# Scores of two tiles in one bank per head, weight blocks that wait for step 8 of the down product, and pooling steps that leave out one product's slot

## The chip, the cores and the metric

The kernel runs on one core of a Trainium2 chip. The metric is the device time of one execution in microseconds (us), as the median of several runs. The core's engines are TensorE (PE in the profile; PEld is its weight load), VectorE (DVE), ScalarE (ACT), GpSimd (POOL) and SyncE (SP), which here only issues DMAs. TensorE's results go to eight banks of PSUM, 512 fp32 numbers per partition each.

## What is computed

One decoder layer on 1024 tokens of width 1024, all in fp32 (cut to its structure):

```python
h = x + 0.5 * swiglu(rms_norm(x, ffn1_norm), w1, w3, w2)          # inner width 2816
u = rms_norm(h, mix_norm)
proj = u @ w_in                       # q, k, v: 768 each; pool: 512; two gates: 1024 each
y_attn = dilated_mixture_attention(q, k, v) @ w_branch_attn       # 3 groups x 4 heads of 64
y_pool = multiscale_pool(pz, pool_w, pool_scale) @ w_branch_pool  # trailing means over 2, 4, 8, 16
merged = sigmoid(gate_a) * y_attn + sigmoid(gate_b) * y_pool
h = h + merged @ w_out
h = h + 0.5 * swiglu(rms_norm(h, ffn2_norm), w1, w3, w2)
return rms_norm(h, final_norm)
```

The attention works on blocks of 128 queries against their own block of keys and the block before it, in three groups of dilation 1, 4 and 16. The three groups' outputs are combined by their softmax denominators.

## The kernel before

Every number is split into a rounded high part (`hi`) and the rest (`lo`), and each product of two numbers is three matmuls, hi by hi, hi by lo and lo by hi (`three`). ScalarE makes the high parts, VectorE and POOL the low parts. The large matrix products are done with seven products of half-size matrices in place of eight, on sums and differences of the quarters. `ORDER` gives the order of the seven products: 1, 6, 2, 7, 5, 4, 3. The order in which instructions are issued is written out by hand: each engine runs its own instructions in the order of the program, and waits for the others by semaphores.

The stages follow each other: entry and first FFN's up product, its down product, the projection `w_in` (the mix stage), attention with the pooling branch's product in between, merge and `w_out`, and the second FFN.

**Down product** (`Down`, lines 727 to 860). The seven products are cut into six steps each, 42 in all; a step multiplies one or two blocks of 128 rows for four tiles of tokens, as `d_f` (line 814). The left side of a step, `g_f`, are sums that the up product has put into DRAM (`gs_f`); `load` (line 753) brings a step's sums back three steps ahead. `begin`, two steps ahead, splits the sums into `ahi_f` and `alo_f` and the weights into `bhi_f` and `blo_f` (`split`, lines 767 and 771). Every fourth low part is POOL's. The right side are blocks of the weights `w2`, or sums and differences of two blocks (`s_f1w`, `s_f2w`, line 789).

The blocks come through a `Stream` (lines 42 to 92): a list of pieces that are loaded in order as soon as `room` says so. Most pieces share a ring of seven tiles `raw`. The pieces numbered in `APART` (13, 14, 22, 23, 37 and 38) have places apart, in the two spare tiles `g`, and `room` allows two of them at a time. A piece that finds no room holds up all pieces behind it.

**Mix stage** (lines 1058 to 1460). It makes 19 outputs in turn, `MIX`: for each of the three groups two halves of q and k and one of v, then gates with two pooling items between them. Each output is seven products `u_mixm` (line 331). In slot `k` of the main loop the operands of product `k + 2` are made, product `k` is issued, and the result of product `k - 1` is taken from its bank by `Mix.out` (lines 1082 to 1101; `y_m`). Results 1 and 5 are taken ahead of the operands. Finished outputs and the split of late weights go on as jobs in the list `later`: at the end of a slot each job that is due does one step, up to its next `yield`, and says how many slots to wait. The job of a pooling item is `window` (lines 1167 to 1210): running sums (`pw`), subtraction of the token, split into `pd_hi` and `pd_lo` (lines 1192 and 1193), then the group's product `pm` (line 1200) and the store.

**Attention** (lines 1605 to 1900). 48 tiles, each of two heads by 128 queries, go in 24 iterations `q` of two tiles. An iteration issues, on PE: the scores `s` of both tiles (line 1624), the transposes `tp` of the exponents of iteration `q - 1` (line 1671), a piece of the pooling branch's product `yp` (line 1763), the values' product `o` of iteration `q - 2` (line 1704). VectorE gathers `o` of `q - 3` (line 1727), masks and reduces the scores (line 1642, `e<-s,mask`) and makes the low part of the transposed exponents (`elo`, line 1686); ScalarE does the exponents (line 1651) and the high part (`ehi`, line 1683). In four of the later iterations `house` also advances the combination of the first two heads (`combine`, lines 1736 to 1744): PE transposes the factors into a bank `fa` (line 1605), VectorE multiplies the gathered outputs by it (`o<-o,fa`, line 1736).

Four banks have the tag `mm` and four the tag `acc`, and each tag's banks are given out in rotation. `s` and `fa` take banks of `mm`; `tp`, `yp`, `o` of the values' product and `pm` take banks of `acc`. A tile of scores takes two banks, one for each head, and uses 128 or 256 of the 512 columns of each.

Of the kernel before, what the change touches and what calls it, by code (L numbers as in the profile page):

```python
# [16 lines left out]
P = 128  # L17
# [8 lines left out]
HD = 64  # L26
SC = HD ** -0.5
GROUPS = 3
# [18 lines left out]
class Stream:  # L47


    def __init__(self, nc, pool):  # L50
        self.nc, self.pool = nc, pool
        self.pieces, self.tiles = [], {}
        self.depth = self.n_loaded = self.n_used = self.n_back = self.end = 0
        self.apart, self.n_apart = set(), 0

    def room(self):
        if self.n_loaded in self.apart:
            return self.n_apart < 2
        return self.n_loaded - self.n_apart < self.n_back + self.depth
# [78 lines left out]
def tile_block(  # L138
# [69 lines left out]
    raws = Stream(nc, keep)  # L208
# [515 lines left out]
    class Down:  # L724
# [3 lines left out]
        def __init__(self, name, sums, half_tile, pair):  # L728
# [7 lines left out]
            self.right, self.apart = {}, set()  # L736
            downs.append(self)

        def size(self, i):
# [81 lines left out]
        def run(self, pool, after, tick=None):  # L821
# [6 lines left out]
            for i, (m, s) in enumerate(self.steps):  # L828
# [23 lines left out]
                if i + 3 < n:  # L852
                    self.load(i + 3)
                if i + 2 < n and not ahead:
                    self.begin(i + 2)
# [396 lines left out]
    ring = {}  # L1252
# [161 lines left out]
    with tc.manual_schedule():  # L1414
# [4 lines left out]
        for k in range(len(items) + 4):  # L1419
# [12 lines left out]
            if k - 1 in results:  # L1432
                q, m = items[k - 1]
                mixes[q].out(m, results.pop(k - 1))
                if m == 3:
                    later.append([k, mixes[q].finish()])
            for job in list(later):
                if job[0] <= k:
                    wait = next(job[1], 0)
                    job[0] = k + wait  # L1440
                    if not wait:
                        later.remove(job)
# [170 lines left out]

    def scores(s):
        hp, g, i = slots[s]
        u = hp * GROUPS + g
        n = blocks(g, i)
        ks = slice((i + 1 - n) * P, (i + 1) * P)
        ps = [bank("mm", f"s{s}_{a}")[:, :n * P] for a in range(2)]
        (qhi, qlo, _), (khi, klo, _) = ring[u]  # L1620
        for j, (l, r) in enumerate(three((qhi, qlo), (khi, klo))):
            for a in range(2):
                rows = slice(a * HD, (a + 1) * HD)
                pe.matmul(ps[a], l[rows, i * P:(i + 1) * P], r[rows, ks], start=(j == 0), stop=(j == 2))
        T[s] = {"s": ps}

# [235 lines left out]
    with tc.manual_schedule():  # L1862
# [8 lines left out]
        for q in range(N // 2):  # L1871
            send()
            scores(2 * q)
            scores(2 * q + 1)
            if q == 0:
# [460 lines left out]
```

## Time and profile before

| | |
|---|---|
| median of 3 runs | 1901.11 us (1900.65 to 1902.72) |
| profiled execution, its own time | 1900.85 us |
| its span in the profile | 1899.1 us |
| mean granted TensorE clock | 0.999 |
| HBM read, written | 229.61 MB, 99.55 MB |
| PE matmuls | 8822 |

Times in the profile count from the start of the span. The execution's own time has 1.75 us more than the span. In the table of busy times each engine has its busy time, its share of the span and its number of instructions. A row of the timeline has start, duration, engine, line, operation, `out<-in`, shapes and a count of like rows taken together; in brackets stands how long the engine was idle just before it, and on whose signal that ended. The shape `128*128 128x512` of a matmul is its weights and its output. Matmuls run pipelined, so a row's duration is longer than the distance to the next one's start.

### The profile page before, as it was taken

Reading aid. Unit: us, or ns where it says so; the run is one execution under the profiler, and the core shown is the slowest. Engines: PE = TensorE matmul, PEld = TensorE weight load, DVE = VectorE, ACT = ScalarE, POOL = GpSimd, SP = SyncE. Lnnn points to the kernel's source line nnn. Section 1 sums busy time; section 2 is a strip of 40 time slices with the busy share of each in tenths; the row PEclk is TensorE's granted clock in tenths of the full one; section 3 lists DMA queues with packets and bytes.
Section 4 is the critical chain, followed back from the end, with each engine's and each line's share of the span. In section 5 each row is a group of like instructions: output and inputs, shape, how many; then the busy total and the mean of one; then the engine's idle time right before and its main releaser. Section 6 shows DMA issues by size and latency. Waiting matters only on the chain. (4 is left out here: it accounts for less than half of the span.)

```text
span 1899.1 us, 24689 instructions
## 1 busy us (share of the span) xinstructions
PE 1884.7 (99%) x8822; PEld 1563.3 (82%) x8822; DVE 1337.4 (70%) x1975; ACT 773.6 (41%) x1394; POOL 718.7 (38%) x533
## 2 busy tenths in 40 slices
PE   9999999999999999999999999999999999999998
PEld 8888888888788888888888888888888888888886
DVE  6776556557886777658886787787665566577867
ACT  7323323333434543334445762363333323334344
POOL 5433333331323354445545456543333333313221
PEclk9999999999999999999999999999999999999999
DMA  5254223336465526765578968644432223354654
GB/s 190 62 199 162 84 89 116 128 117 230 148 228 204 183 89 217 239 213 196 207 254 307 314 212 282 267 153 150 143 127 105 84 103 119 134 197 156 224 195 144
DMA packets 144019, 330.78 MB, mean 174 GB/s; under 512 B 17560, under 2 KB 39064, under 8 KB 142360
## 3 DMA queue, kind: packets, MB, share of 16 engines
q1 hardware_dynamic: 140152, 318.36, 48.6%
q10 hardware_dynamic: 3744, 10.85, 1.5%
q8 instruction: 69, 1.13, 0.2%
q14 instruction: 54, 0.44, 0.1%
HBM read 229.61 MB, written 99.55 MB: 173 GB/s over the span
## 5 line engine op out<-in xcount | busy, mean ns | idle before, releaser
L814 PE MATMUL d_f<-bhi_f,alo_f 128*128 128x512 f32 x616 | 240.1, 390 | 1.4 <-POOL alo_f L771 1.2
L814 PE MATMUL d_f<-bhi_f,ahi_f 128*128 128x512 f32 x616 | 240.3, 390 | 0.0
L814 PE MATMUL d_f<-blo_f,ahi_f 128*128 128x512 f32 x616 | 239.7, 389 | 0.0
L771 POOL TENSOR_TENSOR alo_f<-g_f,ahi_f 128x512 fp32r<-128x512 f32 x60 | 90.0, 1516 | 268.1 <-ACT ahi_f L767 268.1
L331 PE MATMUL u_mixm<-xhi_t_mix,wc_mixm 128*128 128x512 f32 x608 | 157.7, 391 | 0.1
L814 PEld LDWEIGHTS d_f<-bhi_f,alo_f 128*128 128x128 f32 x616 | 115.6, 188 | 26.5 <-POOL alo_f L771 2.6
L814 PEld LDWEIGHTS d_f<-bhi_f,ahi_f 128*128 128x128 f32 x616 | 115.6, 188 | 24.2 <-ACT h L415 0.5
L814 PEld LDWEIGHTS d_f<-blo_f,ahi_f 128*128 128x128 f32 x616 | 115.6, 188 | 23.9
L331 PEld LDWEIGHTS u_mixm<-xhi_t_mix,wc_mixm 128*128 128x128 f32 x608 | 113.4, 188 | 24.0 <-ACT wc_mixm L319 0.6
L331 PE MATMUL u_mixm<-xhi_b_mix,wc_mixm 128*128 128x512 f32 x456 | 120.4, 392 | 0.5 <-DVE y_m L1095 0.5
L322 POOL TENSOR_TENSOR wc_mixm<-s_mixm,wc_mixm 128x512 fp32r<-128x512 f32 x52 | 78.1, 1503 | 109.8 <-ACT wc_mixm L319 103.9
L331 PEld LDWEIGHTS u_mixm<-xhi_b_mix,wc_mixm 128*128 128x128 f32 x456 | 84.8, 188 | 18.1 <-issue 0.9
L319 ACT ACTIVATE wc_mixm<-s_mixm 128x512 fp32r<-128x512 f32 x76 | 47.0, 628 | 110.8 <-DVE s_mixm L373 53.6
L767 ACT ACTIVATE ahi_f<-g_f 128x1024 fp32r<-128x1024 f32 x84 | 81.9, 975 | 11.5 <-DMA g_f<-gs_f 11.5
L331 PE MATMUL u_mixm<-xlo_t_mix,wc_mixm 128*128 128x512 f32 x304 | 81.3, 389 | 0.0
L322 POOL TENSOR_TENSOR wc_mixm<-raw,wc_mixm 128x512 fp32r<-128x512 f32 x40 | 59.3, 1484 | 43.1 <-ACT wc_mixm L319 35.4
L2016 PE MATMUL wo<-w_o,o_hi 128*128 128x512 f32 x224 | 69.3, 390 | 0.0
L767 ACT ACTIVATE bhi_f<-s_f2w 128x512 fp32r<-128x512 f32 x55 | 32.9, 627 | 86.0 <-DVE s_f2w L789 67.1
L767 ACT ACTIVATE bhi_f<-s_f1w 128x512 fp32r<-128x512 f32 x55 | 33.1, 629 | 83.2 <-DVE s_f1w L789 69.9
L331 PEld LDWEIGHTS u_mixm<-xlo_t_mix,wc_mixm 128*128 128x128 f32 x304 | 57.1, 188 | 12.0
L771 DVE TENSOR_TENSOR alo_f<-g_f,ahi_f 128x1024 fp32r<-128x1024 f32 (+1 forms) x48 | 59.7, 1244 | 8.3 <-ACT ahi_f L767 8.3
L331 PE MATMUL u_mixm<-xlo_b_mix,wc_mixm 128*128 128x512 f32 x228 | 61.0, 389 | 0.0
(1332 smaller groups left out, 4758.9 us busy)
## 6 DMA issues: line engine op xcount, KB each, us to landing
g_f<-gs_f SPq DMA_DIRECT2D x70, 512.0 KB
gs_f<-y_f SPq DMA_DIRECT2D x88, 256.0 KB
raw<-in_w2a_dram SPq DMA_DIRECT2D x35, 512.0 KB
raw<-in_w2b_dram SPq DMA_DIRECT2D x35, 512.0 KB
gs_f<-gb_f SPq DMA_DIRECT2D x46, 256.0 KB
raw<-in_w1a_dram SPq DMA_DIRECT2D x22, 512.0 KB
raw<-in_w3a_dram SPq DMA_DIRECT2D x22, 512.0 KB
raw<-in_w1b_dram SPq DMA_DIRECT2D x22, 512.0 KB
```

The lines of the kernel that those rows point to most:

```text
L319: ac.activation(w[:, 0], src, AF.Copy)
L322: eng.tensor_tensor(w[:, 1], src, w[:, 0].bitcast(F32), op=OP.subtract)
L331: pe.matmul(p, a, b, start=(start and n == 0), stop=(n == 11), skip_group_check=not start)
L767: ac.activation(hi[:, c], src, AF.Copy)
L771: eng.tensor_tensor(lo[:, d], src[:, o], hi[:, d].bitcast(F32), op=OP.subtract)
L814: pe.matmul(self.banks[m][t], l, r, start=(first and q == 0), stop=(last and q == 2))
L2016: pe.matmul(banks[m][t], l, r, start=(st == 0 and j == 0 and q == 0), stop=(st == 1 and j == 1 and q == 2))
```

## The change

It has three parts, which don't touch each other.

1. **Scores.** `scores` does both tiles of an iteration and takes one bank per head for the two: the first tile's scores lie in columns 0 to 255 of the bank, the second's in 256 to 511. An iteration takes two banks of `mm` in place of four.
2. **Weight places.** The stream has a number of places for the pieces apart, `places`, in place of the constant 2. A down product sets it to 0 when it begins, and to 2 in step 8 (`len(PAIRS) + 2`, the third step of the second product), where it also calls `load`.
3. **Pooling steps.** A job in `later` also carries its kind, and jobs of the kind `pool` don't advance in the slot that issues a product 5. Each such slot puts off what remains of the job by one slot.

```diff
 class Stream:
-        self.apart, self.n_apart = set(), 0
+        self.apart, self.n_apart, self.places = set(), 0, 0
     def room(self):
         if self.n_loaded in self.apart:
-            return self.n_apart < 2
+            return self.n_apart < self.places
...
 class Down:
             downs.append(self)
+            raws.places = 0
...
                 if i + 3 < n:
                     self.load(i + 3)
+                if i == len(PAIRS) + 2:
+                    raws.places = 2
+                    raws.load()
                 if i + 2 < n and not ahead:
                     self.begin(i + 2)
...
                 if m == 3:
-                    later.append([k, mixes[q].finish()])
+                    later.append([k, mixes[q].finish(), mixes[q].kind])
             for job in list(later):
-                if job[0] <= k:
+                if job[0] <= k and not (job[-1] == "pool" and k < len(items) and items[k][1] == 5):
...
-    def scores(s):
-        hp, g, i = slots[s]
-        u = hp * GROUPS + g
-        n = blocks(g, i)
-        ks = slice((i + 1 - n) * P, (i + 1) * P)
-        ps = [bank("mm", f"s{s}_{a}")[:, :n * P] for a in range(2)]
-        (qhi, qlo, _), (khi, klo, _) = ring[u]
-        for j, (l, r) in enumerate(three((qhi, qlo), (khi, klo))):
-            for a in range(2):
-                rows = slice(a * HD, (a + 1) * HD)
-                pe.matmul(ps[a], l[rows, i * P:(i + 1) * P], r[rows, ks], start=(j == 0), stop=(j == 2))
-        T[s] = {"s": ps}
+    def scores(q):
+
+        banks = [bank("mm", f"s{q}_{a}") for a in range(2)]
+        for s in (2 * q, 2 * q + 1):
+            hp, g, i = slots[s]
+            n = blocks(g, i)
+            ks = slice((i + 1 - n) * P, (i + 1) * P)
+            c0 = s % 2 * 2 * P
+            ps = [b[:, c0:c0 + n * P] for b in banks]
+            (qhi, qlo, _), (khi, klo, _) = ring[hp * GROUPS + g]
+            for j, (l, r) in enumerate(three((qhi, qlo), (khi, klo))):
+                for a in range(2):
+                    rows = slice(a * HD, (a + 1) * HD)
+                    pe.matmul(ps[a], l[rows, i * P:(i + 1) * P], r[rows, ks], start=(j == 0), stop=(j == 2))
+            T[s] = {"s": ps}
...
             send()
-            scores(2 * q)
-            scores(2 * q + 1)
+            scores(q)
```

The changed kernel's lines are 1 higher from the down product on, 4 higher from its `run` on, and 7 higher after `scores`.

**What stands where.** The rows below are instructions of one engine in the order of its program; numbers behind a name tell buffers apart, and the brackets tell on which engines or DMA queues the instruction waits. First PE in an iteration with a combination, before: the transposes of the factors, then the scores of the two tiles (`s_0_9945` and `s_1_9946`, then `s_0_9953` and `s_1_9954`).

```order
L1605 MATMUL fa_1_0_9938<-ident,f_of_9865 128x128 [waits DVE_49,Pool_49]
L1605 MATMUL fa_1_0_9938<-ident,f_of_9865 128x128 x3
L1624 MATMUL s_0_9945<-qk_1_hi,qk_0_hi 128x128 [waits DVE_49]
L1624 MATMUL s_1_9946<-qk_1_hi,qk_0_hi 128x128 [waits DVE_49]
L1624 MATMUL s_0_9945<-qk_1_in,qk_0_hi 128x128
L1624 MATMUL s_1_9946<-qk_1_in,qk_0_hi 128x128
L1624 MATMUL s_0_9945<-qk_1_hi,qk_0_in 128x128
L1624 MATMUL s_1_9946<-qk_1_hi,qk_0_in 128x128
L1624 MATMUL s_0_9953<-qk_1_hi,qk_0_hi 128x128 [waits DVE_49]
L1624 MATMUL s_1_9954<-qk_1_hi,qk_0_hi 128x128 [waits DVE_49]
```

The same place of PE in the changed kernel.

```order
L1609 MATMUL fa_1_0_9900<-ident,f_of_9829 128x128 [waits Pool_49]
L1609 MATMUL fa_1_0_9900<-ident,f_of_9829 128x128 x3
L1631 MATMUL s_0_9907<-qk_1_hi,qk_0_hi 128x128 [waits DVE_49]
L1631 MATMUL s_1_9908<-qk_1_hi,qk_0_hi 128x128 [waits DVE_49]
L1631 MATMUL s_0_9907<-qk_1_in,qk_0_hi 128x128
L1631 MATMUL s_1_9908<-qk_1_in,qk_0_hi 128x128
L1631 MATMUL s_0_9907<-qk_1_hi,qk_0_in 128x128
L1631 MATMUL s_1_9908<-qk_1_hi,qk_0_in 128x128
L1631 MATMUL s_0_9907<-qk_1_hi,qk_0_hi 128x128
L1631 MATMUL s_1_9908<-qk_1_hi,qk_0_hi 128x128
```

The order of the matmuls is the same; the second tile's scores go to the first's banks and wait for nothing of their own, and `fa` no longer waits for VectorE. Before, the banks that the second tile waited for were those of the `fa` rows just above.

Second, SyncE in the first FFN's down product, before, from the sums of step 6 on (`gs_f_0_168`; those of step 7 are `gs_f_2_169`, of step 11 `gs_f_10_173`).

```order
L753 DMA g_f_3847<-gs_f_0_168 128x1024 [waits DMAHW6_49,DMAHW0_49]
L76 DMA raw_3855<-in_w2a_dram 128x2x512 [waits DMAHW7_49,DMAHW2_49,DVE_49]
L76 DMA raw_3857<-in_w2a_dram 128x2x512
L76 DMA raw_3859<-in_w2a_dram 128x2x512 [waits Pool_49]
L753 DMA g_f_3889<-gs_f_2_169 128x1024 [waits DMAHW4_49]
L1338 DMA rope<-in_c_rope_dram 128x768 [waits DMAHW5_49,PE_49]
L753 DMA g_f_3915<-gs_f_4_170 128x1024 [waits DMAHW6_49,DMAHW3_49,Pool_49]
```

The same place of SyncE in the changed kernel.

```order
L754 DMA g_f_3847<-gs_f_0_168 128x1024 [waits DMAHW6_49,DMAHW0_49]
L76 DMA raw_3855<-in_w2a_dram 128x2x512 [waits DMAHW7_49,DMAHW2_49,DVE_49]
L754 DMA g_f_3885<-gs_f_2_169 128x1024
L1342 DMA rope<-in_c_rope_dram 128x768 [waits PE_49]
L754 DMA g_f_3911<-gs_f_4_170 128x1024 [waits DMAHW4_49,DMAHW3_49,Pool_49]
L754 DMA g_f_3952<-gs_f_6_171 128x1024 [waits DMAHW6_49,DMAHW5_49,DVE_49]
L754 DMA g_f_3988<-gs_f_8_172 128x1024 [waits DMAHW0_49,Activation_49,Pool_49]
L754 DMA g_f_4025<-gs_f_10_173 128x512 [waits DMAHW7_49,DMAHW4_49,DVE_49]
L76 DMA raw_4027<-in_w2a_dram 128x2x512
L76 DMA raw_4029<-in_w2a_dram 128x2x512 [waits DMAHW1_49]
L754 DMA g_f_4065<-gs_f_0_144 128x1024 [waits DMAHW2_49,DMAHW5_49,Activation_49,Pool_49]
```

One block still goes ahead of the sums of step 7; the other two have moved behind those of step 11, and stand ahead of those of step 12 (`gs_f_0_144`).

Third, VectorE at the last of the four pooling groups (`pw_1`, `pd_lo`), before; `y_m_1_8295` at line 1091 is the result of product 7 and at line 1095 that of product 5.

```order
L1193 TENSOR_TENSOR pd_lo<-pw_1_8048,pd_hi 128x512 [waits DMAHW1_49,Activation_49]
L382 TENSOR_TENSOR s_mixm_8277<-raw_8021,s_mixm_8160 128x512
L1091 TENSOR_TENSOR y_m_1_8295<-u_mixm_8251,y_m_0_8207 128x512 [waits DMAHW6_49,PE_49]
L1193 TENSOR_TENSOR pd_lo<-pw_1_8048,pd_hi 128x512 [waits Activation_49]
L1095 TENSOR_TENSOR y_m_1_8295<-u_mixm_8282,y_m_1_8295 128x512 [waits DVE_49,PE_49]
L322 TENSOR_TENSOR wc_mixm_8300<-raw_8179,wc_mixm_8300 128x512 [waits DMAHW1_49,Activation_49]
```

The same place of VectorE in the changed kernel.

```order
L382 TENSOR_TENSOR s_mixm_8273<-raw_8015,s_mixm_8160 128x512
L1095 TENSOR_TENSOR y_m_1_8291<-u_mixm_8249,y_m_0_8207 128x512 [waits DMAHW0_49,PE_49]
L1099 TENSOR_TENSOR y_m_1_8291<-u_mixm_8278,y_m_1_8291 128x512 [waits DVE_49,PE_49]
L322 TENSOR_TENSOR wc_mixm_8294<-raw_8179,wc_mixm_8294 128x512 [waits DMAHW1_49,Activation_49]
L1197 TENSOR_TENSOR pd_lo<-pw_1_8069,pd_hi 128x512 [waits DMAHW6_49,Activation_49]
L1242 TENSOR_TENSOR raw_8113<-raw_8113,raw_8177 128x512 [waits DMAHW5_49,DMAHW2_49,DMAHW0_49]
L369 TENSOR_TENSOR s_mixm_8316<-raw_8267 128x512 [waits DMAHW4_49]
L373 TENSOR_TENSOR s_mixm_8318<-s_mixm_8316,raw_8179 128x512 [waits DVE_49]
L1102 SCALAR_TENSOR_TENSOR y_m_1_8291<-u_mixm_8298,y_m_1_8291 128x512 [waits PE_49]
L1197 TENSOR_TENSOR pd_lo<-pw_1_8069,pd_hi 128x512 [waits Activation_49]
```

Both low parts have moved: they stand behind the results of products 7 and 5, with the next product's work between them.

## Prediction

> **What bounds the kernel now.** I read the page's busy times first, then busy time by stretches of the program, then the list of waits, and last the rows of TensorE around the few places where it stands. The first fence is the page's busy line; then come rows of the view by stretches (stretch, its length, PE, PEld, DVE, ACT and POOL busy, granted clock, DMA share, GB/s).
>
> ```profile
> PE 1884.7 (99%) x8822; PEld 1563.3 (82%) x8822; DVE 1337.4 (70%) x1975; ACT 773.6 (41%) x1394; POOL 718.7 (38%) x533
> ```
> ```profile
> 450.00:500.00 50.00, 48.77 (x218) 39.89 (x217) 33.79 (x36) 19.52 (x25) 15.18 (x9) 1.00 0.52 177
> 950.00:1000.00 50.00, 49.50 (x218) 40.56 (x218) 41.07 (x52) 22.11 (x40) 24.65 (x16) 1.00 0.70 248
> 1100.00:1150.00 50.00, 49.13 (x367) 42.50 (x366) 43.10 (x138) 31.77 (x104) 25.03 (x25) 1.00 0.63 200
> 1150.00:1200.00 50.00, 50.00 (x230) 41.40 (x229) 31.41 (x41) 10.92 (x12) 41.65 (x28) 1.00 0.89 320
> 1700.00:1750.00 50.00, 49.85 (x220) 40.95 (x219) 34.16 (x40) 19.59 (x25) 12.77 (x8) 1.00 0.54 184
> ```
>
> TensorE is the bound: 1884.7 of 1899.1 us, so only 14.4 us are idle in the whole program, and the clock is at 1.00 in all these stretches. The change removes no matmul, so it can gain only where PE stands still, and those are the stretches of 48.77, 49.50, 49.13 and 49.85 in place of 50. A loss has no such ceiling: whatever comes late on any engine is seen on PE at once.
>
> Busy time understates the stalls. A matmul's row is longer than the distance to the next one's start, because matmuls are pipelined, so I measure a stall from start to start, less the distance that is usual.
>
> **The change part by part.**
>
> *Weight places, first FFN.* These are rows of PE in the second product of the down projection (start, duration, engine, line, operation, and in brackets the idle time with its releaser), and of the last pooling group's product, which also gives the usual distance.
>
> ```profile
> 476.23 0.40 PE L814 MATMUL d_f<-blo_f,ahi_f 128*128 128x512 f32 x1
> 477.86 0.51 PE L814 MATMUL d_f<-bhi_f,alo_f 128*128 128x512 f32 x1 [1.23 <-POOL alo_f L771]
> ```
> ```profile
> 992.72 0.39 PE L1200 MATMUL pm<-pd_lo,pool_w 128*128 128x512 f32 x1
> 992.95 0.39 PE L1200 MATMUL pm<-pd_hi,pool_w 128*128 128x512 f32 x1
> 993.83 0.47 PE L331 MATMUL u_mixm<-xhi_b_mix,wc_mixm 128*128 128x512 f32 x1 [0.50 <-DVE y_m L1095]
> ```
>
> The usual distance of 512 columns is 992.95 - 992.72 = 0.23 us. The stall at 477.86 is 1.63 - 0.23 = 1.40 us. It is charged to POOL, but POOL is not the cause, as the next rows show: the DMA issues on SyncE's queue, ScalarE's rounding, POOL's low part.
>
> ```profile
> 462.64 1.41 SPq L76 DMA_DIRECT2D raw<-in_w2a_dram  x3
> 464.10 0.47 SPq L753 DMA_DIRECT2D g_f<-gs_f  x1
> ```
> ```profile
> 467.24 1.06 ACT L767 ACTIVATE bhi_f<-raw 128x1024 fp32r<-128x1024 f32 x1 [1.45 <-PE d_f L814]
> 473.16 1.06 ACT L767 ACTIVATE ahi_f<-g_f 128x1024 fp32r<-128x1024 f32 x1 [4.86 <-DMA g_f<-gs_f]
> ```
> ```profile
> 474.30 3.50 POOL L771 TENSOR_TENSOR alo_f<-g_f,ahi_f 128x512 fp32r<-128x512 f32 x2 [9.04 <-ACT ahi_f L767]
> ```
>
> ScalarE stood 4.86 us for the sums of step 7. They were issued at 464.10 behind three weight blocks, and landed at about 473.16: four transfers of 512 KB, 2 MB, in 10.5 us. The change puts two of the three blocks behind the sums of step 11, so 1 MB stands there instead. If the transfers go in order, the sums land after half of 10.5 us, at 467.9. ScalarE is then free at 467.24 + 1.06 = 468.30, ahi ends at 469.36, POOL's two halves at about 472.9, and PE needs the second half at 476.23 + 0.23 = 476.46: 3.5 us to spare. The other end: if the transfers share the rate with each other and with the next sums in the queue, two blocks less save less than half. But the chain from landing to PE is fixed, so 1.40 us earlier, a landing by 471.8, is enough, and that is an eighth of 10.5 us for half of the bytes. So the whole **1.40 us** goes, and what is late next is the following step's sums, which move up in the same queue.
>
> *Weight places, second FFN.* The same program on the second set of weights.
>
> ```profile
> 1717.02 0.39 PE L814 MATMUL d_f<-blo_f,ahi_f 128*128 128x512 f32 x1
> 1717.56 0.50 PE L814 MATMUL d_f<-bhi_f,alo_f 128*128 128x512 f32 x1
> ```
>
> 0.54 - 0.23 = **0.31 us**, with the same cause, so it goes too.
>
> What the two blocks cost in their new place is the unknown of this part. They leave behind the sums of step 11; these rows show that issue and the first use of the late blocks on VectorE.
>
> ```profile
> 478.91 0.32 SPq L753 DMA_DIRECT2D g_f<-gs_f  x1
> ```
> ```profile
> 496.71 1.28 DVE L789 TENSOR_TENSOR s_f1w<-raw,raw 128x512 f32<-128x512 f32 x2
> ```
>
> From 479.2 to 496.71 are 17.5 us for 1 MB, which at the rate above (2 MB in 10.5) takes 5.3 and at half that rate 10.5. The lower bound is a small gain (fewer transfers at once), the upper the stall moved to step 12's sums, which now have 1 MB ahead of them: at most the same 1.40 us per FFN. I take 0, as the queue is empty there but for one transfer of sums per step, and keep 1.4 for the range. SyncE issues nothing else that waits behind them.
>
> *Pooling steps.* From the fence above, the stall at 993.83 is 0.88 - 0.23 = 0.65 us. It waits for the fifth product's result, and VectorE's rows tell why that is late:
>
> ```profile
> 991.72 1.37 DVE L1193 TENSOR_TENSOR pd_lo<-pw,pd_hi 128x512 fp32r<-128x512 f32 x1 [0.68 <-ACT pd_hi L1192]
> 993.01 0.68 DVE L1095 TENSOR_TENSOR y_m<-u_mixm,y_m 128x512 f32<-128x512 f32 x1
> ```
>
> VectorE first stood 0.68 for ScalarE, then did the pooling's low part for 1.37, and only then the result. After the change that low part comes behind the result, so the result starts at about 991.04 and ends at 991.72, before 992.95 + 0.23 = 993.18, when PE wants its bank. **0.65 us** goes. The pooling products (three matmuls per half) come one or two products later on PE. Each low part still stands two products ahead of them on VectorE (a product is 12 matmuls of 0.23, so 5.5 us for two). The two bounds of this move: 0.65 gained, or up to 0.65 lost again at the place where a low part now falls. I take the first, because the pooling rows stand at only four groups, and VectorE is 41.07 of 50 busy there. The stores of the pooling groups go out one or two products later on SyncE's queue, behind those of the gates and late weights; they are loaded again only at the end of this stage.
>
> *Scores.* These are PE's rows of the four iterations in which the combination of the first heads (line 1736) runs, and of one without it.
>
> ```profile
> 1117.69 0.32 PE L1624 MATMUL s<-qk_hi,qk_hi 64*128 64x128 f32 x1
> 1118.28 0.32 PE L1624 MATMUL s<-qk_hi,qk_hi 64*128 64x128 f32 x1 [0.27 <-DVE o L1736]
> 1121.81 0.85 PE L1624 MATMUL s<-xlo_b_mix 64*128 64x256 f32 x2
> ```
> ```profile
> 1122.28 0.38 PE L1624 MATMUL s<-xhi_b_mix,xlo_b_mix 64*128 64x256 f32 x1
> ```
> ```profile
> 1127.19 0.28 PE L1624 MATMUL s<-xlo_b_mix,xhi_b_mix 64*128 64x256 f32 x2
> 1127.54 0.38 PE L1624 MATMUL s<-xlo_b_mix 64*128 64x256 f32 x1
> 1128.14 0.38 PE L1624 MATMUL s<-xlo_b_mix 64*128 64x256 f32 x1 [0.21 <-DVE o L1736]
> ...
> 1132.95 0.78 PE L1624 MATMUL s<-xlo_b_mix 64*128 64x256 f32 x2
> ```
> ```profile
> 1133.35 0.38 PE L1624 MATMUL s<-xhi_b_mix,xlo_b_mix 64*128 64x256 f32 x1
> ```
> ```profile
> 1138.17 0.28 PE L1624 MATMUL s<-xlo_b_mix,xhi_b_mix 64*128 64x256 f32 x2
> ...
> 1138.52 0.28 PE L1624 MATMUL s<-xlo_b_mix,xhi_b_mix 64*128 64x256 f32 x2
> ```
>
> Undisturbed, a pair of heads follows the last after 0.35 / 3 = 0.12 us. The four iterations stand 0.59 - 0.12 = 0.47 (from the second tile's first head to its second), 1122.28 - 1121.81 - 0.12 = 0.35, then 0.35 - 0.12 and 0.60 - 0.12 = 0.71, then 1133.35 - 1132.95 - 0.12 = 0.28: together 1.81 us. The second tile's scores take the banks that `fa` has just left, and these are free only when VectorE has multiplied by them. With two tiles in one bank per head, an iteration needs two banks; those of `fa` come round one iteration later, and the scores' own banks hang on masks long done. So the wait goes.
>
> What is late next are the transposes `tp`, which wait for ScalarE's exponents of the iteration before. The last of the four is the tightest:
>
> ```profile
> 1138.73 1.09 PE L1671 MATMUL tp<-ident,e 128*128 128x128 f32 x8
> ```
> ```profile
> 1137.72 0.50 ACT L1651 ACTIVATE e<-e,stats 128x256 f32<-128x256 f32 x1
> ```
>
> PE would reach it at 1138.73 - 1.81 = 1136.92, and its second half, which holds the last exponents, half of 1.09 later, at about 1137.4. The exponents end at 1138.22 now. They follow VectorE's masks, and VectorE stands for `fa` at these two places of the four iterations:
>
> ```profile
> 1121.53 0.69 DVE L1736 TENSOR_TENSOR o<-o,fa 128x512 f32<-128x512 f32 x1 [0.55 <-PE fa L1605]
> ```
> ```profile
> 1132.60 0.69 DVE L1736 TENSOR_TENSOR o<-o,fa 128x512 f32<-128x512 f32 x1 [0.29 <-PE fa L1605]
> ```
>
> The first wait shrinks by the 0.47 that PE is early by then, the second goes: masks and exponents come 0.76 earlier, the last exponents at 1137.46. So the bounds are all 1.81, or 0.76 if VectorE and ScalarE set the pace throughout. I take 0.1 given back, by these rows: **1.7 us**.
>
> The first pair of tiles, at the start of this stage, has the same wait once:
>
> ```profile
> 1035.91 0.85 PE L1624 MATMUL s<-qk_hi,qk_hi 64*128 64x256 f32 x2
> 1036.38 0.50 PE L1624 MATMUL s<-qk_in,qk_hi 64*128 64x256 f32 x2
> ```
>
> That is 0.47 - 0.12 = 0.35 us. I count nothing for it, because the transposes behind it wait for the first exponents, ahead of which ScalarE loads their table. It stays on the good side of the range.
>
> *The sum.* 1.40 + 0.31 + 0.65 + 1.7 = 4.06 us, say 4.1. The profiled execution took 1900.85 (span 1899.1 and 1.75 around it), so 1896.75; it lies 0.26 below the median 1901.11, so the forecast against the median is **1897.0 us**. What a measurement of this kernel can tell from no change is about 0.2%, 3.8 us: faster means below 1897.31, slower above 1904.91. The forecast lies just beyond the edge.
>
> **The rivals.**
>
> *The gain of the scores is given back.* Behind the attention comes the merge, where the DMA share is 0.89 over 50 us and POOL 41.65 of 50 busy. If PE arrives 1.7 us early and meets transfers that don't, or if the exponents set the pace, only 2.36 us stay: 1898.7. For it: VectorE is 43.10 of 50 busy from 1100 on. Against it: PE has no idle time from 1150 to 1200, and the merge's transfers are issued by events of VectorE and POOL that move along. Chance 0.2.
>
> *The down product's stall is not the weights'.* If the sums of step 7 are slow by themselves, 1.71 us stays: 1898.7 again. For it: nothing shows this transfer alone. Against it: the weights stand right ahead of it. Chance 0.1.
>
> *Slower: the shared bank chains PE and VectorE.* Now the first tile's masks wait for the whole bank, so for the second tile's six matmuls, three distances or 0.35 us later, in each of 24 iterations. If every one were on the chain, 8.4 us come on top: 1905.4. It decides where VectorE reaches a mask before the scores are done. The row for that:
>
> ```profile
> DVE e L1642 <- PE s L1624: 2.1, 2, 1.9
> ```
>
> VectorE waited for scores at 2 of 96 masks, so at most two iterations pay, 0.7 us, and both are at the start. Chance 0.04. [...]
>
> *New stalls of late weights or late pooling.* The 1.4 us of the weights' bound in one FFN, or the 0.65 lost again: 1898 to 1899.5. Chance 0.06.
>
> *More than forecast.* The first pair's 0.35 and smaller waits before the transposes: 1896.3. Chance 0.1.
>
> **How the numbers follow.** The forecast case, 1896.5 to 1897.6, has the remaining 0.5. From 1895.9 to 1899.3 reaches past all cases except the slower one and parts of the last ones, with some half a microsecond for the median's own spread, and leaves out less than 0.2. Faster gets 0.7 of the forecast case and the case of more, 0.45 in all; the rivals that give back and the rest of the forecast make 0.5 within 0.2%; 0.05 slower, the chained bank and what I don't see.
>
> **What would show it.** Right: no PE idle for POOL's low part in the second product of either FFN, the ahi of step 7 at 468 to 471; the fifth result ahead of the pooling's low part and no wait for it; the four iterations of the combination without waits of `s` for `o`. Wrong: a wait of PE for `s_f1w` or for a later low part in the third product of the down projection, of `pm` for `pd_lo`, of `tp` for the exponents in those four iterations, or VectorE's masks waiting for `s` many times.

## The result and the profile after

| | before | after |
|---|---|---|
| median | 1900.65 us (1899.41 to 1902.72, 9 runs) | 1895.32 us (1895.22 to 1896.55, 9 runs) |
| profiled execution | 1900.85 us | 1895.31 us |
| its span | 1899.1 us | 1893.0 us |

The ratio is 0.9973, with a 95% interval of 0.9963 to 0.9983. The change is faster by 5.3 us. The forecast was 1897.0, or 4.1 less than its median of 1901.11; its direction was right, and the time lies below the range, which ended at 1895.9.

The page's busy line and the stretches that were shown of before:

```profile
PE 1882.3 (99%) x8822; PEld 1562.6 (83%) x8822; DVE 1334.6 (70%) x1975; ACT 773.5 (41%) x1394; POOL 711.6 (38%) x533
```
```profile
450.00:500.00 50.00, 50.00 (x225) 41.48 (x224) 34.70 (x38) 21.50 (x28) 12.92 (x9) 1.00 0.53 180
950.00:1000.00 50.00, 50.00 (x222) 41.41 (x221) 41.77 (x52) 23.07 (x41) 27.39 (x16) 1.00 0.67 239
1100.00:1150.00 50.00, 49.84 (x373) 43.12 (x372) 43.63 (x131) 30.79 (x100) 25.84 (x25) 1.00 0.62 199
1150.00:1200.00 50.00, 50.00 (x222) 41.19 (x221) 33.36 (x44) 11.36 (x12) 42.53 (x29) 1.00 0.94 338
1700.00:1750.00 50.00, 50.00 (x223) 41.39 (x222) 37.97 (x45) 20.89 (x28) 13.86 (x10) 1.00 0.53 175
```

All four stretches are full or nearly so, and the merge behind the attention (1150 to 1200) has no idle PE either, though it now starts 4.5 us earlier. PE's busy time also fell, by 2.4 us with the same 8822 matmuls: the rows beside a stall are longer (0.51 us for 0.40) and stand further apart (0.34 us for 0.23, shown below), and that counts as busy.

The down product. Rows of SyncE, ScalarE and POOL for the sums of step 7:

```profile
463.09 0.46 SPq L754 DMA_DIRECT2D g_f<-gs_f  x1
```
```profile
468.44 1.06 ACT L768 ACTIVATE ahi_f<-g_f 128x1024 fp32r<-128x1024 f32 x1 [0.17 <-DMA g_f<-gs_f]
```
```profile
469.57 2.54 POOL L772 TENSOR_TENSOR alo_f<-g_f,ahi_f 128x512 fp32r<-128x512 f32 x2 [4.30 <-ACT ahi_f L768]
```

ScalarE waited 0.17 us in place of 4.86, and starts at 468.44 (forecast: free at 468.30 and the sums there at 467.9). POOL is done at 472.1. The two late blocks were wanted by VectorE at about 495 (its next sums of blocks start at 494.97, with no wait for a DMA).

The mix stage. VectorE's rows at the last pooling group:

```profile
988.20 0.69 DVE L1099 TENSOR_TENSOR y_m<-u_mixm,y_m 128x512 f32<-128x512 f32 x1 [1.23 <-PE u_mixm L331]
988.81 0.68 DVE L322 TENSOR_TENSOR wc_mixm<-raw,wc_mixm 128x512 fp32r<-128x512 f32 x1
990.11 0.69 DVE L1197 TENSOR_TENSOR pd_lo<-pw,pd_hi 128x512 fp32r<-128x512 f32 x1 [0.62 <-ACT pd_hi L1196]
```

The fifth result now waits for PE and not PE for it, and the low part comes behind.

The attention. PE's rows of an iteration with a combination (the second of the four), then the transposes behind the last of them, with ScalarE's last exponents ahead of them:

```profile
1118.47 0.27 PE L1631 MATMUL s<-xlo_b_mix,xhi_b_mix 64*128 64x128 f32 x2
1118.58 0.33 PE L1631 MATMUL s<-xlo_b_mix 64*128 64x256 f32 x2
1118.75 0.28 PE L1631 MATMUL s<-xhi_b_mix,xlo_b_mix 64*128 64x256 f32 x2
```
```profile
1133.61 1.65 PE L1678 MATMUL tp<-ident,e 128*128 128x128 f32 x8
```
```profile
1134.17 0.50 ACT L1658 ACTIVATE e<-e,stats 128x256 f32<-128x256 f32 x1
```

The second tile's first scores follow after 0.11 and 0.17 us, where it was 0.47. But the eight transposes take 1.65 us for 1.09 before: their weight loads wait for the exponents, 0.29 us at 1134.32 and 0.29 again at 1134.81. This is the wait that the prediction named as the next one, and listed among its signs of being wrong; it took 0.1 us for it.

### The profile page after: what moved, and what is told of

Read it like the earlier page. It is cut to its first block, busy times and chain, and to the rows that moved or that the text cites. A ratio compares the mean times of both kernels' runs of the same rounds, so it can differ in the third digit from the quotient of the medians.

```text
span 1893.0 us, 24690 instructions
## 1 busy us (share of the span) xinstructions
PE 1882.3 (99%) x8822; PEld 1562.6 (83%) x8822; DVE 1334.6 (70%) x1975; ACT 773.5 (41%) x1394; POOL 711.6 (38%) x533
## 3 DMA queue, kind: packets, MB, share of 16 engines
q8 instruction: 69, 1.13, 0.2%
## 4 chain that ended last, share of the span: by engine, by line
PE 54%; DVE 2%; ACT 2%; issue 1%; POOL 1%; DMA 0%; ACTq 0%; SPq 0%; DVEq 0%; POOLq 0%
PE u_mixm L331 15%; PE d_f L815 8%; PE wo L2022 4%; PE yp L1770 2%; PE ya L1836 1%; PE u_f20b L331 1%; PE u_f21a L331 1%; PE u_f210b L331 1%; PE u_f210a L331 1%; PE u_f29b L331 1%; PE u_f29a L331 1%; PE u_f28a L331 1%; PE u_f27b L331 1%; PE u_f27a L331 1%; PE u_f26b L331 1%
## 5 line engine op out<-in xcount | busy, mean ns | idle before, releaser
L772 POOL TENSOR_TENSOR alo_f<-g_f,ahi_f 128x512 fp32r<-128x512 f32 x60 | 85.8, 1447 | 270.1 <-ACT ahi_f L768 270.1
```

The source lines that it names most:

```text
L772: eng.tensor_tensor(lo[:, d], src[:, o], hi[:, d].bitcast(F32), op=OP.subtract)
```

## The experiments

To see where time goes below the scatter of the medians I compare traces: the n-th matmul of each name in one trace with the n-th in the other. Below, "in the trace" means this comparison, good to a few hundredths of a microsecond. The start of the last matmul of all is the sum of it:

| profile | last matmul starts | less than before |
|---|---|---|
| before | 1890.42 | |
| the change | 1885.51 | 4.91 |
| places alone | 1888.37 | 2.05 |
| scores alone | 1888.45 | 1.97 |
| pooling alone | 1891.18 | -0.76 |
| before again | 1890.86 | -0.44 |
| one piece of `yp` first | 1887.34 | 3.08 |
| all pieces of `yp` first | 1889.24 | 1.18 |

### Each part alone

The kernel before with one part of the change's diff at a time.

> The kernel before with the weight places alone. Theory A (the prediction's: a stall is the delay of the first matmul behind it): 1.40 + 0.31 = 1.71 us less up to the last matmul. Theory B (a stall also stretches the distances of the matmuls next to it, which the rows of before show as 0.34 for 0.23 right behind 477.86): 2.2 us less, 1.73 in the first FFN and 0.48 in the second. Rival (the sums are late by themselves): 0. The sums of step 7 should be at ScalarE by 468 to 469 in place of 473.16.

Measured: median 1898.60 (1898.07 to 1899.73) against 1900.51 for before in 27 runs on the same chip, ratio 0.9992 with an interval of 0.9983 to 1.0001. This interval does not exclude no change, so the trace has to decide. There the matmuls are 1.72 us earlier behind step 7 of the first FFN and 0.45 us more behind that of the second, of which 0.17 is given back near the end. Theory B holds, A is too small, and the rival is out.

> The kernel before with the scores' banks alone. Theory A: 1.7 us less up to the last matmul (1.8 at the four iterations, 0.1 given back). Theory B: 1.9 us less, made of 2.5 to 2.6 at the four iterations and 0.5 to 0.6 given back to the transposes that wait for the exponents right behind them. Rival (VectorE and ScalarE set the pace): 0.8 us. Rival (shared bank chains PE and VectorE): VectorE waits for scores in many of the 96 masks, and the time is higher.

Measured: median 1899.29, ratio 0.9994, 0.9985 to 1.0003. Again the trace decides. There the four iterations bring 2.57 us, the transposes behind them give back 0.56, and 2.0 stay. Theory B again. The start of the stage gained 0.5 and gave all of it back within 4 us, as the prediction had it. VectorE's waits for the scores, here of the changed kernel:

```profile
DVE e L1649 <- PE s L1631: 2.8, 3, 1.7
```

It is 3 masks in place of 2 of 96. The chain of PE and VectorE through the shared bank did not come about: VectorE is later than the scores nearly everywhere. Where VectorE is early the wait is there: in the first iteration of the changed kernel the first tile's mask starts at 1033.96, behind the second tile's last scores (1033.64, 0.28 long), where before it started at 1036.24, ahead of them (1036.60, 0.39 long).

> The kernel before with the moved pooling steps alone. Theory A: 0.65 us less up to the last matmul. Theory B: 0.8 us less. Rival (a new wait of the pooling products or of a later result): 0 or more.

Measured: median 1898.43 (1897.58 to 1900.93), ratio 0.9990, 0.9981 to 0.9998. At the pooling group the matmuls gain 0.79 us in the trace, by theory B. Two things did not fit. The profiled execution has its last matmul later than before, by 0.76, and the median is 2.1 us lower, where 0.8 was seen. The first has its cause in step 7 of the down product, which this kernel shares with before. PE's rows there:

```profile
475.60 0.51 PE L814 MATMUL d_f<-bhi_f,ahi_f 128*128 128x512 f32 x1 [0.26 <-ACT ahi_f L767]
475.94 0.39 PE L814 MATMUL d_f<-blo_f,ahi_f 128*128 128x512 f32 x1
476.96 0.50 PE L814 MATMUL d_f<-bhi_f,alo_f 128*128 128x512 f32 x1 [0.62 <-POOL alo_f L771]
477.29 0.39 PE L814 MATMUL d_f<-bhi_f,ahi_f 128*128 128x512 f32 x1
477.52 0.40 PE L814 MATMUL d_f<-blo_f,ahi_f 128*128 128x512 f32 x1
479.17 0.50 PE L814 MATMUL d_f<-bhi_f,alo_f 128*128 128x512 f32 x1 [1.25 <-POOL alo_f L771]
```

Three stalls stand where the profile of before has a small one and a large one, since the sums reached ScalarE later in this execution (474.49 for 473.16): 1.28 us more. This stall, which hangs on a transfer, differed from execution to execution. The scatter of the runs does not show it by itself: pooling alone, which has this stall, scatters over 3.4 us, but scores alone, which has it too, over 1.7, as places alone does without it.

### Before once more

> The kernel before once more, unchanged, for a second profile. The profiled executions of before and of the change differ by 5.54 us, of which 4.91 lie ahead of the last matmul's start and some 0.6 to 1.2 behind it. Theory C: what is behind it, the landing of the last stores, differs from execution to execution by about 1 us, so this profile shows a time from the last matmul's start to the end of the span that is not the 8.7 of the first. Rival: it is again 8.7, and the change shortens the end. The stall at step 7 of the down product should vary too, since it is a transfer's landing, by some tenths.

Measured: 1900.89 us. From the last matmul's start to the end of the span are 8.2 us in place of 8.6 (the 8.7 above took the rounded span), so that stretch does scatter, by 0.4. The stall at step 7 is 0.2 us longer. But a part of the end does not scatter. From the issue of the last store to the last packet of it the traces have 2.98 to 2.99 us in before, before again, places alone and scores alone, and 2.20 us in the change and in pooling alone. The stretch from the last matmul to that issue goes from 3.7 to 4.9 us over all profiles of this document, with no order by kernel. So theory C is half right, and the moved pooling steps seem to shorten the very end by 0.8 us, though they lie 900 us ahead of it.

### What the pooling steps have to do with the end

The difference in the traces is a fetch of code. These rows are what the DMA engines moved, in GB/s, in 40 slices of 5.1 us that hold the last store, and the row of a queue that loads code (q14), which a window without a fetch does not have; first before (window 1894.0 to 1899.1), then the change (1888.9 to 1894.0). Under each stands the issue of the last store.

```profile
GB/s 353 418 337 113 337 369 386 418 353 177 0 161 402 369 418 321 402 322 434 386 402 337 129 0 16 0 32 16 32 0 0 0 0 0 0 0 0 0 0 0
...
q14 instruction: 1, 0.01, 0.4%
```
```profile
1894.78 0.34 ACTq L2213 DMA_DIRECT2D out_dram<-n  x1
```
```profile
GB/s 418 337 305 177 353 402 369 402 337 65 0 321 353 418 353 418 354 402 353 418 353 338 32 0 0 0 0 0 0 0 0 0 0 0 0 0 0 0 0 0
```
```profile
1889.64 0.34 ACTq L2219 DMA_DIRECT2D out_dram<-n  x1
```

In before one block of 8 KB of code comes in 1.7 us after that issue, and behind it a few packets trickle on (the 16s and 32s at the end of the row); in the change there is none, and the transfer ends at once. Two packets of the last store, 0.4 and 0.7 us behind the start of the fetch, took 0.29 and 0.23 us, where the others at the end take 0.08 to 0.11, and five more follow them one by one. Moving pooling steps changes how many instructions for semaphores the engines need. Counted with those, POOL has 904 instructions before and 900 after, VectorE 2498 and 2495. So the fetch can have gone past the end of the program with either of them.

> The changed kernel with four tiny fills more on POOL at the start of the program, which do no work for the result. POOL has 900 instructions in the profile of the change and 904 in those without the moved pooling steps. Theory D (the end is longer when POOL's fetch of its next 8 KB of code falls into the last stores, and the moved pooling steps have only pushed it past them by four instructions): the stretch from the last matmul's start to the end of the span goes from 7.5 us back to 8.2 or more, a fetch of code stands within the last 3 us of the span, and the time rises by about 0.9 us. Rival (the moved steps shorten the end in another way, or chance): it stays at 7.5, and so does the time.

> The kernel before with eight such fills more on POOL. Theory D: the fetch of code comes some instructions earlier, ahead of the last store; the stretch from the last matmul to the end goes from 8.2 to 9.1 to about 7.5, and the time falls by about 0.9 us with nothing else changed. Rival: no change of either.

```diff
     warm = consts.tile([P, 1], F32, name="warm")
+    count = consts.tile([P, 1], F32, name="count")
+    for _ in range(4):        # 8 in the second kernel
+        gp.memset(count, 0.0)
```

Measured: 1916.28 and 1920.96 us, ratios 1.0083 (1.0069 to 1.0097) and 1.0106 (1.0093 to 1.0120). They are 21 us slower than the change and than before, which none of the theories had. What is known of that stands in the last section. For the end they still tell: with POOL at 904 the last packet comes 2.19 us after the issue and no fetch lies there, with POOL at 912 and VectorE at 2498 it is 2.98 with a fetch. So POOL's count does not decide, and theory D falls.

> The changed kernel with three tiny fills more on VectorE at the start, into a pad that was there already, so that no address moves. VectorE has 2495 instructions in the profile of the change and 2498 in the profiles whose last stores are late. Theory D2 (it is VectorE's fetch of its next 8 KB of code that falls into the last stores, not POOL's): with 2498 instructions the last store's packets end 2.98 us after its issue in place of 2.20, a fetch of code stands 1.7 us after that issue, and the time rises by about 0.9 us to 1896.2. Rival (another engine's code, or the stores' order by the moved pooling steps): 2.20 again and 1895.3.

> The kernel before with six such fills more on VectorE, 2504 instructions. Theory D2: the fetch comes some instructions earlier, ahead of the last store's issue; the last store's packets end 2.2 us after the issue in place of 2.98, and the time falls by up to 0.9 us, to about 1899.5. Rival: 2.98 again and no change.

```diff
-    consts.tile([P, 24], F32, name="pad")
+    pad = consts.tile([P, 24], F32, name="pad")
...
     ve.memset(mhalf, -0.5)
+    for _ in range(3):        # 6 in the second kernel
+        ve.memset(pad[:, :1], 0.0)
```

Measured: the change with three more instructions on VectorE has a median of 1896.39 us (1895.37 to 1896.69), 1.07 more than the change; before with six more has 1899.95 (1898.80 to 1900.56), 0.68 less than the 1900.63 of before on the same chip; the ratios to before are 0.9977 (0.9968 to 0.9986) and 0.9996 (0.9987 to 1.0005). The same rows, first of the change with three more (window 1889.4 to 1894.5), then of before with six more (1893.3 to 1898.4):

```profile
GB/s 353 418 321 161 305 353 402 369 402 225 0 112 369 386 386 369 370 370 353 450 353 386 177 0 16 0 16 32 32 0 0 0 0 0 0 0 0 0 0 0
...
q14 instruction: 1, 0.01, 0.4%
```
```profile
1890.20 0.34 ACTq L2221 DMA_DIRECT2D out_dram<-n  x1
```
```profile
GB/s 353 418 337 113 337 369 402 353 418 177 0 145 402 337 450 321 434 322 434 337 434 353 145 0 0 0 0 0 0 0 0 0 0 0 0 0 0 0 0 0
```
```profile
1894.09 0.34 ACTq L2215 DMA_DIRECT2D out_dram<-n  x1
```

Three instructions bring the fetch and the trickle back, 2.98 us from issue to last packet; six more take them away from before, 2.20 us. The medians go the same way, but their intervals are too wide to tell 1.07 or 0.68 us from nothing; the traces carry this result. Theory D2 holds for the change: the 0.8 us by which its last store lands sooner come from VectorE's code being three instructions shorter.

VectorE's count is not the whole rule. The two kernels with all pieces of `yp` first and with late places (below) have 2492 and 2495 instructions on VectorE and no fetch on q14 there, and still have 3.03 and 3.06 us. In both, another queue that loads code (q8) has a fetch of 16 KB, 1.5 and 2.7 us ahead of the last store's issue. Rows of the first of them (window 1891.4 to 1896.5):

```profile
GB/s 321 530 193 16 96 289 402 337 402 321 145 305 369 369 402 386 177 32 161 434 337 418 386 370 370 402 369 402 369 145 16 32 16 32 32 16 16 0 0 0
...
q8 instruction: 1, 0.02, 1.1%
```

Over the 14 profiles of this document the eight with a fetch on either queue within 6 us of the last packet have 2.98 to 3.06 us, the six without have 2.19 or 2.20. That the fetch delays the store's packets, on a DMA engine that both would share, is argued from these rows, not shown.

### One weight block ahead

```diff
             downs.append(self)
-            raws.places = 0
+            raws.places = 1
```

> The changed kernel with one place open from the start in place of none, so that one of the two moved weight blocks goes back ahead of the sums of step 7. Theory F (the transfers go in the order of the queue, 0.5 MB in 2.6 us): the sums reach ScalarE at about 471.0, between the 468.4 of the change and the 473.2 of before, and POOL's low part ends within some tenths of the time when PE wants it: a stall of 0 to 0.3 us in place of 1.7. Rival (the transfers share the rate, so that the order decides little): they come hardly later than 468.4 or hardly earlier than 473.

Measured: 1895.66 us, the last matmul at 1885.55 for 1885.51. The rows of ScalarE and POOL:

```profile
470.48 1.06 ACT L768 ACTIVATE ahi_f<-g_f 128x1024 fp32r<-128x1024 f32 x1 [2.03 <-DMA g_f<-gs_f]
```
```profile
471.62 3.53 POOL L772 TENSOR_TENSOR alo_f<-g_f,ahi_f 128x512 fp32r<-128x512 f32 x2 [6.12 <-ACT ahi_f L768]
```

With none, one and two of the two moved blocks ahead the sums reach ScalarE at 468.44, 470.48 and 473.16: 2.0 to 2.7 us for 0.5 MB. Theory F holds, and the packets in the traces say the same: the weights' rows have 2048 bytes and the sums' 4096, and in each of the three traces the packets of 2048 come first and then those of 4096, with an overlap of 1.3 us in before and 1.1 in the change. PE has no stall even at 470.48, so moving one block would have done; this is one execution.

### Places opened too late

```diff
-                if i == len(PAIRS) + 2:
+                if i == len(PAIRS) + 5:
```

> The changed kernel with the places opened in step 11 in place of step 8, in both down products. The bound that the prediction left open: when late weights begin to cost. The blocks are then issued behind the sums of step 14, at about 495 in place of 475, together with two blocks more, 2 MB in 10.5 us by the rate seen so far: they land from 498 on, and VectorE wants the first two at about 495. Expected: a wait of VectorE for them of some 5 us and a stall of PE at step 13 of 0 to 3 us in each down product. If there is none, the change has that much room.

Measured, in one execution: 1903.06 us, 7.7 more than the change, with the last matmul 7.2 us later. Of these 7.2, 1.0 stand ahead of 100 us already, where the two kernels do the same, and 6.4 come in the first FFN's down product. VectorE's row of the late blocks, and three stretches with the granted clock (the eighth number from the left):

```profile
506.06 1.29 DVE L790 TENSOR_TENSOR s_f1w<-raw,raw 128x512 f32<-128x512 f32 x2 [10.03 <-DMA raw<-in_w2a_dram]
```
```profile
500.00:510.00 10.00, 7.63 (x33) 5.64 (x31) 3.78 (x7) 2.12 (x3) 0.95 (x1) 0.98 0.89 298
510.00:520.00 10.00, 9.59 (x29) 7.27 (x30) 9.47 (x14) 4.31 (x6) 2.48 (x3) 0.68 0.47 155
510.00:515.00 5.00, 4.59 (x10) 3.22 (x11) 4.65 (x6) 2.21 (x3) 2.01 (x2) 0.50 0.50 180
```

The blocks were issued from 500.4 on, not at 495, so VectorE waited 10 us and not 5; the second FFN had no such wait. PE stood 2.3 and 0.8 us, and then had a mean clock of 0.68 over ten microseconds, with matmuls 0.43 us apart for 0.23 at first: 29 where 45 go. The clock's fall cost about as much again as the stall (3.3 of the 6.4 us). So step 8 is early enough and step 11 is not.

### Can the transposes' waits be had too

```diff
             if q > 0:
+                next(fill, None)
                 trans_p(q - 1)
                 splits[q - 1] = split_p(q - 1)
-                next(fill, None)
                 if q % 4 != 3:
                     next(fill, None)
```

> The changed kernel with one piece of the pooling branch's product (four matmuls, 0.9 us) ahead of the transposes in each iteration of the attention, in place of behind them. Theory E (the 0.55 us given back behind the combination, and the like waits of 0.2 us at six other iterations, are the transposes waiting for the exponents): the waits of the transposes go, some 1.5 to 1.9 us less up to the last matmul. Rival (ScalarE and VectorE set the pace there): the wait comes back at the values' product or at the next scores, and the time stays within 0.3 us.

Measured: 1896.73 us (1896.26 to 1897.89), ratio to before 0.9981 (0.9972 to 0.9990), 1.4 above the change; in the trace the last matmul is 1.8 us later than the change's. The waits did not go: the transposes' waits add up to 1.4 us where the change has 1.7, and behind the combination three of 0.2 remain. A wait of another kind has come:

```profile
PE o L1711 <- DVE o L1734: 0.3, 1, 0.3
```

> The changed kernel with all pieces of the pooling branch's product of an iteration ahead of the transposes, so that PE changes between kinds of work as often as in the change. Theory G (the run with one piece ahead lost because PE changed kinds of work once more in each of some 20 iterations, 0.08 us each): the transposes' waits for the exponents go without that loss, 1 to 1.5 us less than the change up to the last matmul. Rival (the work on VectorE and ScalarE sets the pace there): new waits at the values' product, time within 0.3 us of the change or above it.

The second piece of the diff then also stands ahead of `trans_p`. Measured: 1898.93 us (1898.48 to 1900.41), ratio to before 0.9993 (0.9984 to 1.0002), 3.6 above the change, with the last matmul 3.7 us later.

```profile
PE o L1711 <- DVE elo L1693: 1.5, 3, 0.5
```

Theory G falls, and E with it. With the transposes later, `ehi` and `elo` are later, and the values' product waits for those. That the loop through exponents, transposes and their low part on ScalarE and VectorE has no room here, so that PE's order only chooses where PE waits, fits these rows but is not shown: the new wait is 1.5 of the 3.7 us, and the rest is not followed. None of the kernels here is faster than the change.

## Why the prediction was wrong in size

In us, with what each part gave in the traces:

| term | forecast | in the change | alone |
|---|---|---|---|
| places, first FFN | 1.40 | 1.72 | 1.72 |
| places, second FFN | 0.31 | 0.45 | 0.45 |
| pooling steps | 0.65 | 0.79 | 0.79 |
| scores | 1.7 | 1.9 | 2.0 |
| up to the last matmul | 4.06 | 4.91 | |
| from the last matmul to the end of the span | 0 | 1.13 | |
| outside the span | 0 | -0.50 | |
| profiled execution | 4.06 | 5.54 | |

The forecast missed 1.5 us of the profiled execution's gain. The rest of its miss of 1.7 is the 0.26 by which it lifted the profiled time to the median of the first three runs: over nine runs before has 1900.65, not 1901.11.

**The bound, the places and the signs were right.** PE stood in those four stretches, the stalls there are gone, nothing new waits for late weights or late pooling, and the merge takes the earlier start but for 0.1 us. The time to ScalarE in the down product was right to half a microsecond.

**The size of a stall was taken too small.** The first step that failed is "I measure a stall from start to start, less the distance that is usual": it gave all four terms of the sum too small, 4.06 us where 4.91 were measured. It measures the delay of the first matmul only. These are the rows behind the stall, before:

```profile
477.86 0.51 PE L814 MATMUL d_f<-bhi_f,alo_f 128*128 128x512 f32 x1 [1.23 <-POOL alo_f L771]
478.20 0.40 PE L814 MATMUL d_f<-bhi_f,ahi_f 128*128 128x512 f32 x1
478.43 0.40 PE L814 MATMUL d_f<-blo_f,ahi_f 128*128 128x512 f32 x1
478.67 0.39 PE L814 MATMUL d_f<-bhi_f,alo_f 128*128 128x512 f32 x1
```

The next distance is 0.34, not 0.23: 0.11 us more for each stall. The first half of the same step had a small stall too (475.65 to 475.99, 0.34 again, with 0.05 ahead of it), which the quoted rows did not cover. Together, with some hundredths in the next distances, 1.72 for 1.40. In the scores each of the four iterations lost 0.2 more than counted, 2.57 for 1.81. There the distance taken off was wrong as well: 0.12 us is the distance from pair to pair, but the two heads of a pair start together (0.003 us apart in the trace), and it was a pair that the stall had split. That is 0.12 in each of the four iterations, over half of the error; the rest is longer distances again. Of the 2.57 the transposes took back 0.55 for the 0.1 of the forecast, so it is luck that this term came out near its 1.7.

**The end was carried over unchanged.** This is the second step that failed: "The sum" took the stretch behind the last matmul, and the 1.75 us around the span, as given. That stretch is 1.13 us shorter: 0.24 up to the last store's issue, which lies within that part's scatter, 0.78 in the landing, and 0.12 behind it. The 0.78 come with VectorE's code fetch, which nothing in the prediction looked at. In pooling alone they bring the 0.8 us that PE gained to 1.6 of the 2.1 by which its median fell; the other 0.5 is within the medians' noise. I could have seen the fetch in the last slices of the profile of before, but not that three instructions less would move it past the end; that needed a count with the semaphore instructions.

The medians of the parts add up, in part by luck: the three alone are 1.9, 1.2 and 2.1 us below before, 5.2 in all, and the change is 5.2 below the same 27 runs; but each carries an interval of some 1.7 us either way, and 1.2 and 2.1 stand half a microsecond and more off the 2.0 and 1.6 of their traces. The range left out both errors because its low end came from stalls alone (the 0.35 of the first pair and the median's spread).

Still open: the span became 6.0 us shorter and the execution only 5.5, as 2.3 us lie outside the span after the change for 1.8 before. No run here tells what they hold. The traces give a hint: the five profiles with no fetch of code behind the span have 1.8 us outside it, the nine with one have 1.9 to 2.3. So a fetch that is pushed past the end may give back a part of what it saved.

## What to carry to other kernels

Price a stall by the whole stretch until the matmuls have their usual distance again, not by the first late start; here that was a fifth more, and take off the distance that these very matmuls have undisturbed. Where a wait hangs on a transfer, move what stands ahead of it in the same queue: its landing moves by the bytes (here 2.0 and 2.7 us for 0.5 MB). When a change of a few microseconds is judged, look at the end of the program too: instructions that come or go elsewhere can move a fetch of code into or out of the last store (here three fills at the start, on VectorE, took its landing from 2.20 to 2.98 us).

## What the hardware did that was not expected

- **A new tile of four bytes, or its fills.** The two kernels with a new tile of one fp32 number per partition were 21 us slower. The rows of the stretch from 100 to 150 us, first of the change, then of the change with that tile and four fills:

```profile
100.00:150.00 50.00, 50.00 (x222) 41.44 (x221) 39.06 (x54) 15.09 (x26) 19.02 (x13) 1.00 0.61 206
```
```profile
100.00:150.00 50.00, 50.00 (x216) 40.15 (x215) 38.76 (x53) 14.20 (x24) 17.56 (x13) 1.00 0.57 192
```

PE is busy throughout at full clock, and does 216 matmuls in place of 222: 0.2315 us each for 0.2252. This holds in the first FFN's up product (12 us in all) and the mix stage (9), and not in the down products, the attention or the second FFN's up product. The four fills take 0.57 us on POOL at the start, the eight 1.20. The kernels with fills on VectorE into a pad that was there already show no such thing (1896.39 and 1899.95 us). What makes the matmuls slower is not shown: no run had the tile without the fills, and none had fills on POOL without the tile.
- **Clock after a stall.** In the run with late places, 2.3 and 0.8 us without work within four microseconds were followed by a clock of 0.68 over ten. From 510 to 515 us it was 0.50, with matmuls 0.43 us apart for 0.23. Shorter stalls were not followed by such a fall: behind the stall of 1.4 us before the change the clock stayed at 1.00 (450 to 500 us), and pooling alone, with three stalls of 2.6 us in all within some four, has a mean clock of 0.999 over its span, as before has, where late places has 0.997.
